# Second attention of a hybrid decoder layer: compressed product with v, and the first query block's local and selected scores, as 256-column joint matmuls

## The chip, the core and the metric

The kernel runs on one core of a Trainium2 chip. The metric is device time in microseconds for one execution; the figure given for a kernel is the median of its runs. Five engines matter here: PE (the matrix engine, whose weight loads have a row of their own, PEld), DVE (vector), ACT (scalar, with the exponential), POOL (GpSimd, which here also issues some DMAs) and SP (which issues most DMAs).

## What is computed

One decoder layer on 512 tokens of width 1024. Three causal token mixers (called DSA, NSA and SSD) work side by side on a common projection, and their gated sum goes through an output projection and a feed-forward block. The change is in the NSA mixer, the second attention. It has 16 query heads in two groups g = 0, 1 of eight heads, each group with its own keys and values, and for each query it adds three attentions with a gate each:

```python
s = jnp.einsum('bqghd,bngd->bqghn', qb, k_cmp) * scale      # compressed: 31 windows
o_cmp = jnp.einsum('bqghn,bngd->bqghd', p_cmp, v_cmp)
s = jnp.einsum('bqghd,bgqkd->bqghk', qb, k_sel) * scale     # selected: 4 blocks of 64 keys
o_slc = jnp.einsum('bqghk,bgqkd->bqghd', p, v_sel)
s = jnp.einsum('bqghd,bkgd->bqghk', qb, kwb) * scale        # local window of 512 keys
o_win = jnp.einsum('bqghk,bkgd->bqghd', p, vwb)
return gb[..., 0:1] * o_cmp + gb[..., 1:2] * o_slc + gb[..., 2:3] * o_win
```

Queries go in four blocks b = 0 to 3 of 128. Keys after the query are masked, so block b needs 128(b+1) keys. For blocks 0 and 1 the four selected key blocks are all that are visible, so the mask of the selected attention is the causal one there.

## The kernel before

**Number format.** A value that has to be exact is split into a high and a low part (`hi`, `lo`), both in a reduced float32 format, and a product is then the sum of two or three matmuls into one PSUM tile. Projections use three of them (`mm3`, L454 to L457); scores use the keys' two parts against one stationary operand that holds the query (`kh` at L905, `kl` at L906); the products with v use the probabilities' two parts (`ph`, `pl`, L956 and L957).

**The attention units.** The NSA work is a list of 32 units (`nsa_units`, L1112): for each pair (b, g) in the order NORD, which is (3,0), (0,0), (2,0), (1,0), (3,1), (2,1), (1,1), (0,1); for each half j = 0, 1 of a group's eight heads, that is four heads; and for each kind, first "w" (local) and then "s" (selected). The keys of the four kinds are separate tiles `K["s0"]`, `K["s1"]`, `K["w0"]`, `K["w1"]` (L514).

**A unit's steps.** `a1` (L893) computes scores: per head two matmuls of n = 128(b+1) columns, then one DVE instruction that copies them out of PSUM, adds the mask and takes the row maximum (L907); after the four heads one small DVE instruction (L912) and four exponentials on ACT (L914). `a2` (L917) divides by the sum and applies the gate. `b1` (L932) transposes the probabilities on PE, 128 keys at a time for four heads (L944), splits them on ACT and DVE (L948, L949) and multiplies them by v (L956, L957, 512 columns: four heads of 128 queries). A "w" unit opens the PSUM tile `pv`, into which `cmp_pv` (L1104) first puts the compressed attention's product with v: one 128-column matmul for each of the four heads (L1108). The "s" unit of the same half adds to the same tile and closes it.

**The pipeline** (L983) runs, for each unit, `load`, `prep`, `a1` of this unit, `b1` of the unit before, `a2` of this unit. A unit's `load` is where the next pair's work is hung in: the loads of its queries (issued by POOL, L1000), its compressed scores (`cmp_a`, L1036), its selection (`cmp_b`) and its transposed compressed probabilities (`cmp_c`).

**The filler and the order.** A second generator, the filler (L691), makes the projections, the merge gates and the branch projections, which are long rows of 512-column matmuls. Each step of the attention yields a number of nanoseconds, times a ratio (2.5 for NSA), and so much filler is traced before the next step (L1759 to L1777). Instructions of the main generator carry a priority that puts them ahead of filler traced up to some thousand steps before (`HM`, L35). A scheduler then orders every engine's instructions at compile time; on the chip each engine runs its list in that order. Near the end some steps wait in this tracing for each other by name: the "s" units of the last pair need the tile `yC` (L1146), and the filler's last NSA branch needs the marks of those units (L1461 to L1474).

Of the kernel before, what the change touches and what calls it, by code (L numbers as in the profile page):

```python
# [7 lines left out]
F32 = mybir.dt.float32  # L8
# [33 lines left out]
def build_kernel(ctx, tc, A, out):  # L42
# [468 lines left out]
    def r_tile(pl, name, shape):  # L511
        return pl.tile(shape, F32R, name=name)

    K = {n: (r_tile(kv, "kh_" + n, [128, S]), r_tile(kv, "kl_" + n, [128, S])) for n in ("s0", "s1", "w0", "w1")}  # L514
    V = {n: r_tile(kv, "v_" + n, [128, NB, 2, 64]) for n in ("s0", "s1", "w0", "w1")}
    mk = popen("mask", side="right")
    K["d"] = (r_tile(mk, "kh_d", [128, S]), r_tile(mk, "kl_d", [128, S]))
# [375 lines left out]
    def a1(u, ratio):  # L893
# [19 lines left out]
        for h in range(4):  # L913
            act.activation(u.p[h][:, :n], u.p[h][:, :n], AF.Exp, bias=u.nb[:, h:h + 1],  # L914
                           scale=rs8[:, u.b, u.h0 + h:u.h0 + h + 1], accum_out=u.sm[:, h:h + 1])

    def a2(u):  # L917
        n = 128 * (u.b + 1)
        rc = at.tile([128, 4], F32, name="rc", bufs=3)
        dve.reciprocal(rc, u.sm)  # L920
        if u.gate is not None:
            dve.tensor_tensor(rc, rc, u.gate, op=ALU.mult)
        for h in range(4):
            if h == 3:
                if u.gate is not None:
                    act.activation(u.p[h][:, :n], u.p[h][:, :n], AF.Copy, scale=rc[:, h:h + 1])
                else:
                    pool.tensor_tensor(u.p[h][:, :n], u.p[h][:, :n], bc(rc[:, h:h + 1], [128, n]), op=ALU.mult)
            else:
                dve.tensor_scalar(u.p[h][:, :n], u.p[h][:, :n], rc[:, h:h + 1], None, op0=ALU.mult)  # L930
# [52 lines left out]
    def pipeline(units, ratio):  # L983
        prev = None
        for u in units + [None]:
            if u is not None:
                if u.load is not None:
                    yield from u.load()
                u.prep()
                yield from a1(u, ratio)  # L990
            if prev is not None:
                yield from b1(prev, ratio)
            if u is not None:
                a2(u)
            prev = u
# [7 lines left out]
    def y_dst(which, h0, b):  # L1003
        t = y_d[which]
        a = t[h0 * 64:(h0 + 4) * 64, b * 128:(b + 1) * 128]
        return a.rearrange("(h d) q -> d h q", d=64)
# [96 lines left out]

    def cmp_pv(b, g, j):  # L1104
        def pre(o, ratio):
            for h in range(4):
                vh = vz[:, g, h % 2].rearrange("p a b -> p (a b)")
                pe.matmul(o[:, h * 128:h * 128 + 128], vh, PC[b, g][:, 2 * j + h // 2], start=h == 0, stop=False)  # L1108
            yield ratio * 428
        return pre  # L1110

    def nsa_units(ratio):  # L1112
# [46 lines left out]
        for i, (b, g) in enumerate(order):  # L1159
            for j in range(2):  # L1160
                for kind in "ws":
                    u = U()
                    u.b, u.h0 = b, 16 + 8 * g + 4 * j
                    u.k, u.v = K[f"{kind}{g}"], V[f"{kind}{g}"]
                    gi = 2 if kind == "w" else 1
                    u.gate = gate[:, b].rearrange("p (h j) -> p h j", j=3)[:, 8 * g + 4 * j:8 * g + 4 * j + 4, gi]
                    u.first, u.last, u.direct = kind == "w", kind == "s", None
                    u.pre = cmp_pv(b, g, j) if kind == "w" else None
                    u.ydst = y_dst("b", 8 * g + 4 * j, b)

                    def prep(u=u, b=b, g=g, j=j, kind=kind):
                        u.q = Q[b, g][j]
                        u.mask = caus[:, 384 - 128 * b:] if kind == "w" else SM[b, g]
                    u.prep = prep
                    u.load = None
                    if i == 0:
                        u.load = {(0, "w"): lambda: start(0), (0, "s"): second, (1, "w"): lambda: start(1),
                                  (1, "s"): lambda: both(1)}[j, kind]
                    elif j == 0 and kind == "w":
                        u.load = lambda i=i: load(i + 1)  # L1180
                        if i == 1:
                            u.load = lambda i=i: att2(load(i + 1))
                    if i and j == 0 and kind == "s":
                        u.load = lambda i=i: cont(i + 1, cmp_q)
                    if i and j == 1 and kind == "w":
                        u.load = lambda i=i: cont(i + 1, cmp_b)
                    if i == 4 and j == 1 and kind == "w":
                        u.load = lambda i=i: mark(cont(i + 1, cmp_b))
                    if i == 7 and kind == "s":
                        u.load = lambda u=u, j=j: direct(u, j)  # L1190
                    elif i == 6 and j == 1 and kind == "s":
                        u.load = lambda i=i: half(cont(i + 1, cmp_c))
                    elif i and j == 1 and kind == "s":
                        u.load = lambda i=i: cont(i + 1, cmp_c)
                    us.append(u)
# [610 lines left out]
```

## Time and profile before

| | |
|---|---|
| median of three runs | 1375.47 us (1375.29 to 1377.54) |
| profiled execution, first to last instruction | 1374.2 us |
| PE busy | 1352.5 us, 98% |
| DVE, ACT, POOL busy | 1001.6, 723.3, 266.7 us |
| first and last score matmul of NSA (L905) | 546.1 and 923.9 us after the start |
| last product with v of NSA (L957) | 956.4 us after the start |

For the profiled execution the page gives the span alone; the median of the runs is 1.3 us above it. A timeline row has a start, a duration and an instruction. Matmuls are pipelined and their ends are modelled, so what a matmul costs is read from the distance between starts, not from its duration.

### The profile page before, as it was taken

The page shows a single profiled execution, that of the slowest core. Times are in us where ns is not written, and L with a number is a line of the kernel's source. Part 1 is how long each engine was busy: PE and PEld are TensorE (multiplying, and loading weights), DVE is VectorE, ACT ScalarE, POOL GpSimd, SP SyncE. Part 2 cuts the span into 40 slices and gives each one's busy share as a digit, 9 for nine tenths or more (in the row PEclk, how much of TensorE's full clock was granted, in tenths as well). Part 3 has the DMA queues.
Part 4 walks back from the last instruction along what each step waited for, and adds up shares of the span by engine and source line. Part 5 has one row for each costly group of instructions (what it writes and reads, how often), then busy time and mean ns, then how long its engine had stood idle before and what let it go on. Part 6 is the DMA issues. An engine that isn't in the chain of part 4 may idle for free.

```text
span 1374.2 us, 19666 instructions
## 1 busy us (share of the span) xinstructions
PE 1352.5 (98%) x6875; PEld 1129.7 (82%) x6875; DVE 1001.6 (73%) x1968; ACT 723.3 (53%) x1434; POOL 266.7 (19%) x230
## 2 busy tenths in 40 slices
PE   9999999999998999999999999999999999999998
PEld 7888888888886767888888888887989888888887
DVE  6499987989877576876676888987745666767741
ACT  5455345676766675566666566553224344443430
POOL 2425111111027783200000001114101201102000
PEclk9999999999999999999999999999999999999999
DMA  6436555554467886635345454546535665846531
GB/s 196 119 91 156 176 162 157 131 140 119 112 215 237 245 252 182 170 104 146 104 115 154 126 147 115 150 138 191 180 112 165 128 167 124 183 113 132 153 119 50
DMA packets 222592, 205.34 MB, mean 149 GB/s; under 512 B 15369, under 2 KB 169885, under 8 KB 222494
## 3 DMA queue, kind: packets, MB, share of 16 engines
q1 hardware_dynamic: 206524, 180.49, 44.8%
q0 software_dynamic: 15232, 20.98, 8.1%
q10 hardware_dynamic: 738, 2.63, 0.5%
q8 instruction: 54, 0.88, 0.3%
q14 instruction: 44, 0.36, 0.1%
HBM read 167.56 MB, written 36.51 MB: 148 GB/s over the span
## 4 chain that ended last, share of the span: by engine, by line
PE 90%; DVE 3%; POOL 2%; DMA 2%; issue 2%; ACT 1%; SPq 0%; DVEq 0%; POOLq 0%; ACTq 0%
PE pj L455 21%; PE pj L456 21%; PE pj L457 21%; PE sc L457 3%; PE sc L455 3%; PE sc L456 3%; PE pT L944 3%; PE sc L906 2%; PE sc L905 2%; PE pv L956 2%; PE pv L957 2%; DMA E<-ac_d 1%; PE pF L944 1%; PE sc L1330 1%; POOL t L1314 1%
## 5 line engine op out<-in xcount | busy, mean ns | idle before, releaser
L172 ACT ACTIVATE whi<-wraw 128x1024 fp32r<-128x1024 f32 (+2 forms) x190 | 198.4, 1047 | 222.4 <-PE pj L456 109.9
L174 DVE TENSOR_TENSOR wlo<-wraw,whi 128x1024 fp32r<-128x1024 f32 (+1 forms) x176 | 226.0, 1287 | 95.4 <-ACT whi L172 93.8
L455 PE MATMUL pj<-hTh,whi 128*128 128x512 f32 x384 | 153.8, 401 | 0.0
L457 PE MATMUL pj<-hTh,wlo 128*128 128x512 f32 x384 | 153.1, 399 | 0.0
L456 PE MATMUL pj<-hTl,whi 128*128 128x512 f32 x384 | 152.8, 398 | 0.0
L914 ACT ACTIVATE p<-p,nb,rs 128x256 f32<-128x256 f32 (+3 forms) x192 | 123.2, 645 | 38.7 <-DVE nb L912 38.6
L455 PE MATMUL pj<-whi,hTh 128*128 128x512 f32 (+2 forms) x336 | 132.0, 393 | 2.6 <-DVE v_s L556 2.2
L456 PE MATMUL pj<-wlo,hTh 128*128 128x512 f32 (+2 forms) x336 | 131.7, 392 | 0.0
L457 PE MATMUL pj<-whi,hTl 128*128 128x512 f32 (+2 forms) x336 | 131.1, 390 | 0.0
L455 PE MATMUL pj<-yh,whi 128*128 128x512 f32 (+1 forms) x288 | 105.9, 374 | 1.9 <-DVE rtok L1535 0.8
L456 PE MATMUL pj<-yl,whi 128*128 128x512 f32 (+1 forms) x288 | 107.4, 373 | 0.0
L457 PE MATMUL pj<-yh,wlo 128*128 128x512 f32 (+1 forms) x288 | 106.6, 370 | 0.0
L456 PE MATMUL pj<-h2l,whi 128*128 128x512 f32 (+1 forms) x256 | 96.3, 376 | 0.0
L457 PE MATMUL pj<-h2h,wlo 128*128 128x512 f32 (+1 forms) x256 | 96.2, 376 | 0.0
L455 PE MATMUL pj<-h2h,whi 128*128 128x512 f32 (+1 forms) x256 | 96.1, 376 | 0.0
L1000 POOL DMA_DIRECT2D qu<-q_d x32 | 23.5, 735 | 330.8 <-PE sc L906 165.4
L457 PEld LDWEIGHTS pj<-hTh,wlo 128*128 128x128 f32 x384 | 72.2, 188 | 14.6 <-issue 0.7
L456 PEld LDWEIGHTS pj<-hTl,whi 128*128 128x128 f32 x384 | 72.3, 188 | 13.5 <-issue 0.7
L455 PEld LDWEIGHTS pj<-hTh,whi 128*128 128x128 f32 x384 | 72.3, 188 | 13.4 <-issue 0.5
L948 ACT ACTIVATE pth<-pT 128x512 fp32r<-128x512 f32 x95 | 55.0, 593 | 49.7 <-PE pT L944 48.1
L455 PEld LDWEIGHTS pj<-whi,hTh 128*128 128x128 f32 x336 | 64.0, 190 | 15.6 <-DVE v_s L556 2.5
L457 PEld LDWEIGHTS pj<-whi,hTl 128*128 128x128 f32 x336 | 63.8, 190 | 12.0 <-issue 0.5
(403 smaller groups left out, 3265.0 us busy)
## 6 DMA issues: line engine op xcount, KB each, us to landing
wraw<-in_w_in_dram SPq DMA_DIRECT2D x84, 512.0 KB, 4.1
wraw<-in_w_ff_dram SPq DMA_DIRECT2D x58, 512.0 KB, 4.3
qd<-in_w_ff_dram POOLq DMA_DIRECT2D x18, 512.0 KB, 5.9
gld<-g_d SPq DMA_DIRECT2D x35, 256.0 KB, 2.7
q_d<-qev SPq DMA_DIRECT2D x64, 128.0 KB, 2.5
qu<-q_d POOLq DMA_DIRECT2D x32, 256.0 KB, 3.8
E<-ac_d SPq DMA_DIRECT2D x16, 512.0 KB, 6.0
xz<-xz_d SPq DMA_DIRECT2D x16, 512.0 KB, 6.0
```

The source lines that it names most:

```text
L172: act.activation(hi[:, :m], r[:, :m], AF.Copy)
L174: (pool if i in LOWP else dve).tensor_tensor(lo[:, :m], r[:, :m], f(hi[:, :m]), op=ALU.subtract)
L455: pe.matmul(o, lh, rh, start=first, stop=False)
L456: pe.matmul(o, lh, rl, start=False, stop=False)
L457: pe.matmul(o, ll, rh, start=False, stop=last)
L905: pe.matmul(s_[:, h % w, :n], u.q[h], kh[:, :n], start=True, stop=False)
L906: pe.matmul(s_[:, h % w, :n], u.q[h], kl[:, :n], start=False, stop=True)
L914: act.activation(u.p[h][:, :n], u.p[h][:, :n], AF.Exp, bias=u.nb[:, h:h + 1], scale=rs8[:, u.b, u.h0 + h:u.h0 + h + 1], accum_out=u.sm[:, ...
L944: pe.transpose(pt[:, h], u.p[h][:, kb * 128:kb * 128 + 128], ident)
L948: act.activation(ph, ptf, AF.Copy)
L956: pe.matmul(o, vk, ph0, start=st, stop=False)
L957: pe.matmul(o, vk, pl0, start=False, stop=en)
```

## The change

Three edits go together.

1. The keys of a group's local and selected attention are laid side by side in one tile, `KJ[g]`, shape 128 x 2 x 512; `K["w0"]` and so on become views of it.
2. For block b = 0, where either kind has 128 keys, the "w" unit calls `a1_two` in place of `a1`: per head two matmuls of 256 columns (128 local and 128 selected keys, two runs 512 elements apart), then two DVE instructions, one for each kind; after the four heads the small DVE instruction and the four exponentials of the "w" unit, then those of the "s" unit. The "s" unit is marked `ready` and skips `a1`. The yields of the two units' scores, 4 x 2 x 2 x 107 ns before the ratio, become 4 x 240 ns.
3. `cmp_pv` makes two matmuls of 256 columns in place of four of 128: two heads that share a stationary operand (the even ones, the odd ones) go together, their output in two runs of 128 columns, 256 apart.

```diff
-    K = {n: (r_tile(kv, "kh_" + n, [128, S]), r_tile(kv, "kl_" + n, [128, S])) for n in ("s0", "s1", "w0", "w1")}
+    KJ = [(r_tile(kv, f"kh_j{g}", [128, 2, S]), r_tile(kv, f"kl_j{g}", [128, 2, S])) for g in range(2)]
+    K = {f"{n}{g}": tuple(t[:, i] for t in KJ[g]) for i, n in enumerate("ws") for g in range(2)}
...
+    def a1_two(u, v, ratio):
+        for w in (u, v):
+            for n in ("mx", "nb", "sm"):
+                setattr(w, n, at.tile([128, 4], F32, name={"sm": "smx"}.get(n, n), bufs=3))
+            t = at.tile([128, 4, 128], F32, name="p", bufs=PB)
+            w.p = [t[:, h] for h in range(4)]
+        for h in range(4):
+            if h % 2 == 0:
+                s_ = ps("sc", [128, 2, 2, 128])
+            for i, k in enumerate(u.two):
+                pe.matmul(s_[:, h % 2], u.q[h], k[:, :, :128], start=i == 0, stop=i == 1)
+            for i, w in enumerate((u, v)):
+                dve.tensor_tensor_reduce(w.p[h], s_[:, h % 2, i], caus[:, 384:], 1.0, -3.4e38, ALU.add, ALU.max,
+                                         accum_out=w.mx[:, h:h + 1])
+            yield ratio * 240
+        rs = rs8[:, u.b, u.h0:u.h0 + 4]
+        for w in (u, v):
+            dve.scalar_tensor_tensor(w.nb, w.mx, -1.0, rs, op0=ALU.mult, op1=ALU.mult)
+            for h in range(4):
+                act.activation(w.p[h], w.p[h], AF.Exp, bias=w.nb[:, h:h + 1], scale=rs[:, h:h + 1], accum_out=w.sm[:, h:h + 1])
...
-                yield from a1(u, ratio)
+                if getattr(u, "two", None) is not None:
+                    yield from a1_two(u, units[units.index(u) + 1], ratio)
+                elif not getattr(u, "ready", False):
+                    yield from a1(u, ratio)
...
-            for h in range(4):
-                vh = vz[:, g, h % 2].rearrange("p a b -> p (a b)")
-                pe.matmul(o[:, h * 128:h * 128 + 128], vh, PC[b, g][:, 2 * j + h // 2], start=h == 0, stop=False)
+            o4 = o.rearrange("p (k e q) -> p e k q", k=2, e=2)
+            for e in range(2):
+                vh = vz[:, g, e].rearrange("p a b -> p (a b)")
+                pe.matmul(o4[:, e], vh, PC[b, g][:, 2 * j:2 * j + 2], start=e == 0, stop=False)
...
+                    u.two = KJ[g] if b == 0 and kind == "w" else None
+                    u.ready = b == 0 and kind == "s"
...
-                        u.mask = caus[:, 384 - 128 * b:] if kind == "w" else SM[b, g]
+                        u.mask = caus[:, 384 - 128 * b:] if kind == "w" or u.ready else SM[b, g]
```

## The prediction

> **What bounds the kernel now.** I read the page's first part, then the table by stage, then the list of what PE waited for while the second attention (NSA) runs.
>
> ```profile
> span 1374.2 us, 19666 instructions
> PE 1352.5 (98%) x6875; PEld 1129.7 (82%) x6875; DVE 1001.6 (73%) x1968; ACT 723.3 (53%) x1434; POOL 266.7 (19%) x230
> ```
> ```profile
> core 0: us, PE busy (x) PEld busy (x) DVE busy (x) ACT busy (x) POOL busy (x), PEclk, DMA share, GB/s
> 545.00:600.00 55.00, 54.96 (x282) 45.56 (x280) 41.86 (x102) 31.84 (x63) 13.39 (x6) 1.00 0.59 163
> 600.00:640.00 40.00, 40.00 (x214) 33.62 (x214) 26.70 (x83) 22.86 (x49) 0.71 (x1) 1.00 0.40 110
> ...
> 880.00:940.00 60.00, 60.00 (x301) 49.93 (x300) 48.26 (x122) 34.31 (x82) 11.24 (x8) 1.00 0.52 154
> 940.00:1000.00 60.00, 58.12 (x343) 50.82 (x342) 44.06 (x69) 18.37 (x25) 14.55 (x9) 1.00 0.62 206
> ```
> ```profile
> PE pj L455 <- DVE rtok L1535: 0.8, 1, 0.8
> PE pj L455 <- ACT yh L820: 0.7, 1, 0.7
> PE pj L455 <- DVE gld L1535: 0.4, 1, 0.4
> PE pj L455 <- DVE x L1564: 0.3, 1, 0.3
> ```
>
> The third fence is the whole list of PE's waits from 545 to 1010 us: 0.8 + 0.7 + 0.4 + 0.3 = 2.2 us. PE's busy time alone would prove little, since the ends of matmuls are modelled; the short list does. The attention's short pieces lie inside the filler's long rows of 512-column matmuls, and PE goes from one to the next without a pause. DVE is busy 48.26 of 60 us and ACT 34.31 where the last query blocks run, 26.70 and 22.86 of 40 us where the first pair with b = 0 runs: neither is the bound, nor are the DMAs at 0.40 to 0.62. The granted clock is 1.00. So time in this stage is the sum of what PE's matmuls cost, and one that goes away shortens the kernel wherever in the stage it stands.
>
> **Which matmuls the change touches.** All of line 1108, and those of lines 905 and 906 that have 128 columns and read a kind "w" or "s" key:
>
> ```profile
> L1108 PE MATMUL pv<-cph,vz 128*128 128x128 f32 x64 | 9.6, 267 | 0.0
> ```
> ```profile
> L905 PE MATMUL sc<-kh_w,qu x64: 218/333/478, 546.1 to 912.4; 128*128 128x512 f32 x16, 128*128 128x128 f32 x16, 128*128 128x384 f32 x16, 128*128 128x256 f32 x16
> L905 PE MATMUL sc<-kh_s,qu x64: 220/337/442, 559.3 to 923.9; 128*128 128x512 f32 x16, 128*128 128x128 f32 x16, 128*128 128x384 f32 x16, 128*128 128x256 f32 x16
> ```
> ```profile
> L906 PE MATMUL sc<-kl_w,qu x64: 273/309/400, 546.4 to 912.5; 128*128 128x512 f32 x16, 128*128 128x128 f32 x16, 128*128 128x384 f32 x16, 128*128 128x256 f32 x16
> L906 PE MATMUL sc<-kl_s,qu x64: 273/332/459, 559.5 to 923.9; 128*128 128x512 f32 x16, 128*128 128x128 f32 x16, 128*128 128x384 f32 x16, 128*128 128x256 f32 x16
> ```
>
> That is 64 products with v and 4 x 16 = 64 score matmuls, 128 in all, each of 128 columns. The change replaces them by 64 of 256 columns. Counted in groups of four that become two: 16 groups of products (one for each "w" unit) and 16 groups of scores (a head's four matmuls), 32 groups.
>
> **What a matmul of each width costs.** The durations in these rows (267 ns, 273 ns) hold the passage through the array, which overlaps the next one; the cost is the distance between starts. One place of the timeline has eight of the short ones in a row:
>
> ```profile
> 906.61 0.40 PE L457 MATMUL pj<-yh,wlo 128*128 128x512 f32 x1
> 906.84 0.40 PE L455 MATMUL pj<-yh,whi 128*128 128x512 f32 x1
> 907.07 0.22 PE L905 MATMUL sc<-kh_s,qu 128*128 128x128 f32 x1
> 907.13 0.28 PE L905 MATMUL sc<-kh_w,qu 128*128 128x128 f32 x1
> 907.24 0.28 PE L906 MATMUL sc<-kl_s,qu 128*128 128x128 f32 x1
> 907.36 0.27 PE L906 MATMUL sc<-kl_w,qu 128*128 128x128 f32 x1
> 907.47 0.61 PE L1108 MATMUL pv<-cph,vz 128*128 128x128 f32 x4
> 907.91 0.44 PE L456 MATMUL pj<-yl,whi 128*128 128x512 f32 x1
> 908.20 0.39 PE L457 MATMUL pj<-yh,wlo 128*128 128x512 f32 x1
> ```
>
> A 512-column matmul costs 906.84 - 906.61 = 0.23 us. From 907.07 to 908.20 there are 1.13 us for eight short ones and one long: (1.13 - 0.23) / 8 = 0.1125 us for a short one. The first appears to cost only 0.06 (907.07 to 907.13), but the long one behind the row takes 908.20 - 907.91 = 0.29 instead of 0.23: the 0.06 that were missing are paid there. Something of about 0.11 us that does not depend on the columns goes with each matmul; I read it as the load of its own stationary operand, which each of them has, and which a 512-column matmul hides and a 128-column one does not.
>
> A 256-column matmul stands in the scores of query block 1, between long ones:
>
> ```profile
> 883.46 0.28 PE L905 MATMUL sc<-kh_s,qu 128*128 128x256 f32 x1
> 883.58 0.28 PE L906 MATMUL sc<-kl_s,qu 128*128 128x256 f32 x1
> 883.70 0.39 PE L456 MATMUL pj<-yl,whi 128*128 128x512 f32 x1
> 883.93 0.39 PE L957 MATMUL pv<-ptl,v_s 128*128 128x512 f32 x1
> ```
>
> 883.46 to 883.70 is 0.24 us for two, 0.12 us each, and the long one behind takes its usual 0.23: nothing is left over. So 256 columns cost hardly more than 128.
>
> **The sum.** A group costs 4 x 0.1125 = 0.45 us before and 2 x 0.12 = 0.24 us after: 0.21 us saved. 32 groups: 6.7 us, half of it from the products with v, half from the scores. Against the profiled execution that is 1374.2 - 6.7 = 1367.5 us of span. The median of the runs is 1375.47 - 1374.2 = 1.3 us above the span, and I keep that: 1368.8 us.
>
> The Trainium skill ("TensorE: Matmul & The Clock Gate", section "Back-to-back issue gap") gives for a stream of weight loads and matmuls about 81 ns at 128 columns and 131 ns at 512. With an estimate of 98 ns between them at 256, a group would save 4 x 81 - 2 x 98 = 128 ns and the kernel 4.1 us. The rows above have 112 and 230 ns in their place, and the trace decides.
>
> **What is not on PE.** DVE and ACT keep their instructions: eight mask-and-maximum instructions, two small ones and eight exponentials for the two units, on the same 128 x 128 shapes. Their cost is nothing as long as PE has filler to run, which in this stage it has. No DMA is added. What moves: the "s" unit's four mask-and-maximum instructions and four exponentials now stand ahead of the transposes' copies for the unit before, and behind the "w" unit's first scores. DVE has in queue behind them the copies out of PSUM for `b1`; ACT the other half of these. The loads of the next queries on POOL wait for the last score matmul that reads a query buffer, and that one comes earlier. The keys' joint tile is written long before 545 us, in two parts as before; I cost it at nothing. The smaller yields trace 4 x (428 - 240) x 2.5 = 1880 ns less filler for each of the four joint units; since PE is filled either way, this shifts where filler stands, and I cost it at nothing too. If PE had no filler there, the price would be the rival below.
>
> Two shapes of operands are not in the trace: a moving operand in two runs of 128 columns 512 elements apart (scores), and an output in two runs 256 apart (products). Their bounds are 0.12 us, the 256-column row, and 2 x 0.1125 = 0.225 us, two short matmuls; I take 0.12, as the row of the same count of columns. A gain below 0.12 is excluded to within 0.005, because two such matmuls fill the 0.23 us of one with 512 columns.
>
> **The rivals.**
>
> *The two runs cost what two matmuls cost.* Then 64 x 0.225 us equal 128 x 0.1125 us and nothing is gained: 1375.5. For it speaks only that no row shows such an operand; against it that the 0.11 us go with a matmul's own weights, and one load serves both runs.
>
> *Cost goes by columns.* If the 0.1125 us were an accident of the one row that I read, and a matmul really cost its columns, 0.23 / 512 = 0.45 ns each, then four times 128 columns would be twice 256 columns, 0.23 us both, and nothing would be gained: 1375.5. The 0.06 us between 907.07 and 907.13 is just that rate; the seven distances behind it are double. The same section of the Trainium skill has this rule for a single matmul, columns over 2.4 plus 2.5 ns, 55.8 and 109.2 ns; by it a group would save 5 ns and the kernel 0.2 us, and the trace disagrees with 112 for 128 columns.
>
> *The gain turns into waits on loads.* After NSA the filler's rows wait for y to be fetched and split (the 0.7 and 0.8 us rows above, and 60 - 58.12 = 1.9 us of idle PE from 940 to 1000). If transfers there do not start earlier, PE arrives sooner and waits longer. With these waits doubled, 1.9 us are lost: 1370.7. Against it: the buffers that these transfers need are freed by PE's own progress.
>
> *Slower: the "w" unit's softmax comes late.* Between its scores and its transposes there used to stand the scores of the "s" unit; now the joint scores come first, and the exponentials start only after eight mask-and-maximum instructions in place of four, with eight exponentials ahead of the copies for `b1`.
>
> ```profile
> L907 DVE CUSTOM_DVE_ANT_0 p<-sc,caus 128x128 f32<-128x128 f32 x48 | 13.5, 285 | 13.4 <-PE sc L906 12.9 <-PE pT L944 0.3
> L907 DVE DVE_READ_ACCUMULATOR2_ANT mx<- 128x1 f32 x192 | 15.6, 81 | 0.0
> ```
> ```profile
> L914 ACT ACTIVATE p<-p,nb,rs 128x128 f32<-128x128 f32 x48 | 23.1, 483 | 9.3 <-DVE nb L912 9.3
> ```
>
> Four times 285 + 81 ns are 1.5 us on DVE, four times 483 ns are 1.9 us on ACT, and the 0.9 us of the "s" unit's eight score matmuls no longer lie in between: up to 4.3 us for each of four joint units, 17.2 us, if PE's list puts the transposes where they would have been ready and no filler ahead of them. 1375.5 - 6.7 + 17.2 = 1386.0. It decides from 6.7 / 4 = 1.7 us of PE waiting in each joint unit. For it speaks that PE's order is fixed at compile time; against it that the same kind of wait is absent today: in the list of waits none of PE's is for line 914 or 948, and in the row of line 907 it is DVE that waits for PE.
>
> **How the numbers follow.** I give the forecast 0.72, the gain partly turned into waits 0.09 (two thirds of it still more than 0.2% faster), two runs as two matmuls 0.06, cost by columns 0.04, slower 0.09. About 0.2%, 2.7 us, is what a measurement of this kernel can tell from no change. Faster: 0.72 + 0.06 = 0.78. Same: 0.03 + 0.06 + 0.04 = 0.13. Slower: 0.09. The time is that of the forecast, 1368.8. Downward the range allows for all of the 2.2 us of waits to vanish with the new order (1366.6), and half a microsecond for the widths read to 0.01 us: 1366.0. Upward it reaches to no gain, 1375.5. It leaves out the slower case and the rims of the others, under 2 in 10. The forecast's own range is 1366.0 to 1371.5.
>
> **What would show it right or wrong.** PE should have 64 matmuls fewer, 6811. Line 1108's successor should show two 256-column matmuls in 0.24 us, and the long matmul behind them at 0.23; the joint scores the same. If these distances are 0.2 us or more, the rival of the two runs holds. The list of PE's waits from 545 to 1000 us should stay near 2 us; a row of waits for line 914's successor, for 948 or for 949, of 1.7 us or more per joint unit, would be the slower case. NSA's last product with v and everything behind it should come about 6.7 us earlier, and the stretches before 545 us should be unchanged; a difference there would be a new order, not this change's arithmetic.

## The result and the profile after

The changed kernel takes 1384.72 us (median of four runs, 1382.92 to 1386.15) beside 1375.84 us (1375.29 to 1377.54) for the kernel before on the same chip: a ratio of 1.006, with a 95% interval of 1.0046 to 1.0074. It is slower by 8.9 us, where 6.7 us less had been forecast. The profiled execution took 1384.38 us, 1.7 us more than its span.

The page's first part, and the table by stage for the stretches that the prediction showed:

```profile
span 1382.7 us, 19544 instructions
PE 1354.4 (98%) x6811; PEld 1125.4 (81%) x6811; DVE 996.7 (72%) x1968; ACT 722.2 (52%) x1434; POOL 272.3 (20%) x230
```
```profile
545.00:600.00 55.00, 55.00 (x280) 45.94 (x279) 40.06 (x101) 30.89 (x61) 13.05 (x6) 1.00 0.58 161
600.00:640.00 40.00, 40.00 (x212) 33.63 (x211) 31.22 (x109) 28.61 (x71) 1.43 (x2) 1.00 0.42 119
640.00:880.00 240.00, 237.69 (x1228) 199.62 (x1228) 180.12 (x463) 146.72 (x312) 15.49 (x14) 1.00 0.45 127
880.00:940.00 60.00, 54.86 (x241) 41.40 (x240) 41.26 (x103) 27.61 (x64) 13.90 (x8) 1.00 0.44 133
940.00:1000.00 60.00, 56.73 (x328) 48.85 (x327) 44.73 (x70) 19.42 (x27) 16.47 (x10) 0.97 0.56 183
```

PE has the 64 matmuls fewer (6811). Up to 640 us it is as full as before. From 640 to 880 us it is idle for 2.3 us, and from 880 to 940 us for 5.1; before, it had no idle time at all in either. The row of before for 640 to 880 us, which the prediction does not show:

```profile
640.00:880.00 240.00, 240.00 (x1252) 202.82 (x1251) 186.14 (x477) 148.33 (x316) 16.35 (x16) 1.00 0.46 130
```

The list of PE's waits from 545 to 1010 us had four rows and 2.2 us. Now it has ten (columns as before: total, times, longest):

```profile
PE pj L455 <- ACT yh L821: 4.6, 5, 2.5
PE pv L1134 <- DVE yt L996: 1.3, 1, 1.3
PE pv L978 <- ACT pth L970: 1.2, 2, 0.8
PE pj L455 <- DVE gld L1565: 1.1, 2, 0.8
PE pF L966 <- DVE p L952: 0.9, 1, 0.9
PE pj L455 <- DVE rtok L1563: 0.8, 1, 0.8
PE sc L928 <- DVE mx L930: 0.3, 1, 0.3
PE pj L455 <- DVE x L1592: 0.3, 1, 0.3
PE pv L979 <- DVE ptl L971: 0.2, 1, 0.2
PE pj L456 <- DVE yl L822: 0.2, 1, 0.2
```

Together 10.9 us. The largest row is the filler's: its matmuls (L455) wait for a y tile to be split (L821), which is the first step of a new branch. The matmuls themselves cost what was forecast. Two places of PE's timeline, the joint scores and the joint product:

```profile
612.17 0.40 PE L928 MATMUL sc<-kh_j,qu 128*128 128x256 f32 x2
612.41 0.40 PE L928 MATMUL sc<-kl_j,qu 128*128 128x256 f32 x2
612.65 0.39 PE L978 MATMUL pv<-pth,v_w 128*128 128x512 f32 x1
612.88 0.40 PE L455 MATMUL pj<-hTh,whi 128*128 128x512 f32 x1
...
882.83 0.40 PE L1134 MATMUL pv<-cph,vz 128*128 128x256 f32 x2
883.07 0.40 PE L978 MATMUL pv<-pth,v_w 128*128 128x512 f32 x1
883.30 0.28 PE L928 MATMUL sc<-kh_j,qu 128*128 128x256 f32 x1
```

612.17 to 612.65 is 0.48 us for four, 882.83 to 883.07 is 0.24 us for two: 0.12 us each, and the 512-column matmuls behind keep their 0.23. Of the 64 joint matmuls, 53 are followed by the next matmul after 0.112 to 0.124 us; the distances behind the other 11, 0.149 to 1.06 us, hold waits or leftovers of their neighbours.

**A ledger.** To see where the saving went, I add up matmul widths between 545 us and the end of the first NSA branch (the start of DVE's last merge in it). A matmul of n columns is put at 0.4427 ns a column plus 1 ns, and at 111 ns at least; these fit the distances read in the prediction, 0.23 and 0.1125 us. What the trace takes beyond the sum is called lost: pauses, and slower matmuls. So "attention" is a count of matmuls at fixed prices, and "lost" is all that remains; neither is measured by itself. The filler's branches are, in order, the DSA branch a0, the two halves of SSD c0 and c1, and the first NSA branch b0.

| us | merge gates | a0 | c0 | c1 | b0 | sum |
|---|---|---|---|---|---|---|
| attention, before | 68.5 | 27.3 | 21.1 | 12.3 | 1.4 | 130.5 |
| attention, after | 66.9 | 27.2 | 23.8 | 4.3 | 1.1 | 123.3 |
| lost, before | 1.7 | 0.9 | 0.8 | 1.0 | 1.9 | 6.4 |
| lost, after | 1.8 | 1.9 | 5.3 | 8.7 | 4.8 | 22.5 |

By this count the attention's matmuls take 7.2 us less. The lost time grows by 16.1 us, and 10.6 of these lie in c1 and b0; 16.1 - 7.2 = 8.9 us, 0.4 more than the spans differ by (1382.7 - 1374.2 = 8.5). Behind b0 the time is the same (409.1 us in both), and NSA's first matmul starts at 545.1 us instead of 545.8.

The attention's scores now finish early. The small DVE instruction that ends a unit's scores stands in one row before, in two after:

```profile
L912 DVE SCALAR_TENSOR_TENSOR nb<-mx,rs x32: 147/157/726, 562.3 to 926.1; 128x4 f32<-128x4 f32 x32
```
```profile
L913 DVE SCALAR_TENSOR_TENSOR nb<-mx,rs x24: 106/161/447, 562.4 to 876.4; 128x4 f32<-128x4 f32 x24
L935 DVE SCALAR_TENSOR_TENSOR nb<-mx,rs x8: 144/156/164, 613.6 to 896.4; 128x4 f32<-128x4 f32 x8
```

The last one starts at 896.4 instead of 926.1 us. (The last product with v does not come earlier: it starts in b0, at 964.9 us instead of 956.4.) So in c1 there are 4.3 us of attention where there were 12.3, and where a branch ends and the next one's y is not there yet, PE has nothing else in its list. The longest pause is at the start of b0. SP's, ACT's and PE's rows for it:

```profile
944.94 0.32 SPq L1447 DMA_DIRECT2D gld<-g_d  x1
945.36 0.38 SPq L153 DMA_DIRECT2D wraw<-in_w_br_nsa_dram  x1
945.80 0.97 SPq L820 DMA_DIRECT2D yr<-yb_d  x2
```
```profile
950.17 1.36 ACT L821 ACTIVATE yh<-yr 128x512 fp32r<-128x512 f32 x2 [3.89 <-DMA yr<-yb_d]
```
```profile
947.98 0.40 PE L457 MATMUL pj<-yh,wlo 128*128 128x512 f32 x1
950.85 0.74 PE L455 MATMUL pj<-yh,whi 128*128 128x512 f32 x2 [2.48 <-ACT yh L821]
```

The third and fourth y tile are asked for at 945.80, behind 256 KB of gates and 512 KB of weights, and land 4.3 us later; PE stands from 948.2, where the 0.23 us of the matmul at 947.98 end, to 950.85: 2.65 us. (The row's 2.48 counts from that matmul's modelled end.)

### The profile page after: what moved, and what is told of

Its sections match the earlier page's. It is cut to its first block, busy times and chain, and to the rows that moved or that the text cites. A ratio compares the mean times of both kernels' runs of the same rounds, so it can differ in the third digit from the quotient of the medians.

```text
span 1382.7 us, 19544 instructions
## 1 busy us (share of the span) xinstructions
PE 1354.4 (98%) x6811; PEld 1125.4 (81%) x6811; DVE 996.7 (72%) x1968; ACT 722.2 (52%) x1434; POOL 272.3 (20%) x230
## 4 chain that ended last, share of the span: by engine, by line
PE 79%; DVE 6%; DMA 5%; POOL 4%; ACT 3%; issue 2%; SPq 0%; DVEq 0%; POOLq 0%; ACTq 0%
PE pj L455 19%; PE pj L456 19%; PE pj L457 19%; PE sc L457 3%; PE sc L456 3%; PE sc L455 3%; PE pT L966 2%; PE sc L907 2%; PE pv L978 2%; PE sc L906 2%; PE pv L979 2%; DMA E<-ac_d 1%; DMA yr<-yc_d 1%; POOL E L1318 1%; POOL xz L1330 1%
## 5 line engine op out<-in xcount | busy, mean ns | idle before, releaser
L455 PE MATMUL pj<-hTh,whi 128*128 128x512 f32 x384 | 153.2, 399 | 0.0
L455 PE MATMUL pj<-whi,hTh 128*128 128x512 f32 (+2 forms) x336 | 131.5, 391 | 2.8 <-DVE v_s L557 2.2
L915 ACT ACTIVATE p<-p,nb,rs 128x256 f32<-128x256 f32 (+3 forms) x160 | 107.8, 677 | 42.2 <-DVE nb L913 42.2
L455 PE MATMUL pj<-yh,whi 128*128 128x512 f32 (+1 forms) x288 | 106.6, 375 | 6.5 <-ACT yh L821 4.6
L455 PE MATMUL pj<-h2h,whi 128*128 128x512 f32 (+1 forms) x256 | 96.1, 376 | 0.0
L455 PEld LDWEIGHTS pj<-hTh,whi 128*128 128x128 f32 x384 | 72.2, 188 | 13.6 <-issue 0.5
L455 PEld LDWEIGHTS pj<-whi,hTh 128*128 128x128 f32 x336 | 63.6, 189 | 15.0 <-DVE v_s L557 2.5
```

Source lines behind the costliest of these rows:

```text
L455: pe.matmul(o, lh, rh, start=first, stop=False)
```

## Experiments

All ratios are to the kernel before, run beside it on the same chip, with 95% intervals. "Lost" and "attention" are sums of the ledger, each from the one profiled execution. That one lies up to 2.9 us from the median of its kernel (2.9 above it with the joint scores alone, the slowest of six), so two lost times that differ by less than about 3 us are not told apart.

**First: each part alone, and the yields.** The joint product without the joint scores, as an edit of the kernel before:

```diff
-            for h in range(4):
-                vh = vz[:, g, h % 2].rearrange("p a b -> p (a b)")
-                pe.matmul(o[:, h * 128:h * 128 + 128], vh, PC[b, g][:, 2 * j + h // 2], start=h == 0, stop=False)
+            o4 = o.rearrange("p (k e q) -> p e k q", k=2, e=2)
+            for e in range(2):
+                vh = vz[:, g, e].rearrange("p a b -> p (a b)")
+                pe.matmul(o4[:, e], vh, PC[b, g][:, 2 * j:2 * j + 2], start=e == 0, stop=False)
```

> The kernel before with the joint product with v alone (32 matmuls of 256 columns for 64 of 128); scores and yields as before. Order theory (the smaller yields of the joint scores let the attention run ahead of the filler, so that it is used up where the filler has its gaps): the yields are untouched, so the saving shows in full, 16 x 0.21 = 3.4 us, 1372.4 us. Late-softmax theory (the joint scores with their eight exponentials make PE wait): the same, 1372.4. Any-change theory (each edit gives another order with losses of its own): no saving, 1376 to 1385.

1380.02 us, 1.0015 (1.0006 to 1.0025). The saving of 3.4 us does not show; 13.6 us are lost instead of 6.4.

The joint scores without the joint product, as an edit of the changed kernel:

```diff
-            for e in range(2):
-                vh = vz[:, g, e].rearrange("p a b -> p (a b)")
-                pe.matmul(o4[:, e], vh, PC[b, g][:, 2 * j:2 * j + 2], start=e == 0, stop=False)
+            for h in range(4):
+                vh = vz[:, g, h % 2].rearrange("p a b -> p (a b)")
+                pe.matmul(o[:, h * 128:h * 128 + 128], vh, PC[b, g][:, 2 * j + h // 2], start=h == 0, stop=False)
```

> The changed kernel with the old product with v: joint scores and their small yields alone. Order theory and late-softmax theory alike: all of the loss is here, 1384.7 + 3.4 = 1388 us. Any-change theory: anything between 1372 and 1388.

1388.24 us, 1.0077 (1.0064 to 1.0091). The worst of the four: 0.6 us of attention are left in c1, 25.5 us are lost. The change with the yields of before:

```diff
-            yield ratio * 240
+            yield ratio * 428
```

> The changed kernel with the yield of the joint scores set to 428 per head, so that the two units together yield what the separate ones did. All matmuls are those of the change. Order theory: the attention keeps its old place beside the filler, PE's lost time from 746 to 1000 us goes from 23 us back to about 7, and the time is 1369 us, at most 1373. Late-softmax theory: nothing about the joint scores has changed, 1384 us. Any-change theory: between.

1384.77 us, 1.0053 (1.004 to 1.0066). The last small DVE instruction of the scores still starts at 894.4 us, so the smaller yields are not what makes the scores early; that theory falls. The kernel before, with no matmul touched, and only smaller yields for the scores of block 0:

```diff
-            yield ratio * max(n / 2.4, 107) * 2
+            yield ratio * (120 if u.b == 0 and u.k is not K["d"] else max(n / 2.4, 107) * 2)
```

> The kernel before, its matmuls untouched, but with block 0's NSA scores yielding 120 per head and unit in place of 214, so that the two units together yield the 240 per head of the change. Order theory: the attention runs ahead as in the changed kernel, and the kernel is slower by up to 16 us, 1380 to 1391. Late-softmax theory: no change, 1375.8. Any-change theory: anything from 1373 to 1385.

1383.32 us, 1.0042 (1.0028 to 1.0055): slower by about 5 us with the same work. The two largest of its five rows of waits are of the same kind as the change's largest:

```profile
PE pj L455 <- ACT yh L820: 3.8, 2, 3.4
PE pj L456 <- DVE yl L821: 1.6, 2, 1.4
```

So an edit that only makes the scheduler write a new order can cost more than half of what the change costs (1.0042 beside 1.006), and no joint matmul is needed for that.

**Second: the order held, and the attention held back.** In two kernels every instruction gets its rank in the order of before as its priority:

```diff
-    pe, act, dve, pool = nc.tensor, nc.scalar, nc.vector, nc.gpsimd
+    pe, act, dve, pool = Px(nc.tensor, "T"), Px(nc.scalar, "A"), Px(nc.vector, "V"), Px(nc.gpsimd, "P")
...
+                tc.cur_priority = RANK[key][o] * 8 if FIX[0] is None else FIX[0]
```

> The product with v alone as joint matmuls, and the order of before written into the priorities: every instruction of the program gets its rank in the order of before as its priority in the scheduler, so that the compile-time order stays near that of before (the lists still differ in places). The last attention instructions then stand in the rows of the second SSD branch as before (15.0 us of attention after the first half of the SSD rows by matmul widths; before 12.2 there, counted in the same way). Theory 'cover' (the saving on PE is real, and time is lost where a new order leaves PE's loads of y uncovered): the saving of 3.4 us appears, ratio to before 0.9975, that is 1372 to 1373 us beside 1376. Rival 'any new order loses' (the order of before is a lucky one, and any difference costs): 1.001 to 1.004 as in the run with the joint product alone. Rival 'joint matmuls cost more than they show' (PE time of the joint product is hidden in the modelled ends): no gain, 1.000 or above.

> The whole change (yields of 428 a head), with the order of before written into the priorities as in the run beside it; the mask-and-maximum instructions of the selected kind rank right behind those of the local kind. By matmul widths 10.1 us of attention stand behind the first half of the SSD rows (after the change 4.7, before 12.2). Theory 'cover': the saving of 6.7 us appears less what the joint softmax costs by waiting, ratio 0.995 to 0.998, that is 1369 to 1373 beside 1376. Rival 'any new order loses': 1.003 to 1.006. Rival 'joint softmax late' (the slower rival of the prediction, independent of where the attention stands): 1.000 to 1.005, with PE waits for the lines 930, 942 to 952 of several us.

The product alone: 1381.68 us, 1.003 (1.0018 to 1.0042), 16.9 us lost. The whole change, with its old yields: 1379.26 us, 1.0018 (1.0005 to 1.003), 16.7 lost. Both miss what "cover" expected. They have 11.2 and 9.5 us of attention in c1, and c1 and b0 lose 7.3 and 7.2 us instead of 13.5; but c0 loses 6.6 and 6.7, with new waits of up to 1.7 us of scores for the row maximum that frees their PSUM tile. Here, priorities taken from an order did not give that order.

The other two hold the attention back by one line, once in the change and once in the kernel before:

```diff
+        HI[0] = 400
         yield from pipeline(nsa_units(R2), R2)
```

> The whole change, and one line more: the priority offset of the second attention's instructions is 400 in place of 4000, so that attention pieces are no longer always put ahead of the filler. By matmul widths 15.9 us of attention then stand in the second SSD branch's rows (after 4.7, before 12.2), some of them up to the first NSA branch rows. Theory 'cover': lost time of PE in these stretches falls from 21 us to about 7, ratio to before 0.993 to 0.998 (1367 to 1373 beside 1376). Rival 'any new order loses': 1.003 to 1.006 as for the other new orders. Rival 'joint softmax late': 1.000 to 1.005, with PE waiting for DVE and ACT at the joint units.

> The kernel before, matmuls untouched, with the priority offset of 400 in place of 4000 in the second attention: a new order, with 13.4 us of attention in the second SSD branch's rows (before 12.2), reaching further towards the first NSA branch. Theory 'cover': 0.998 to 1.001, since the cover is the same or a little better. Rival 'any new order loses': 1.003 to 1.006.

The change: 1374.38 us, 0.9981 (0.9969 to 0.9993), faster than the kernel before by 0.2%, about the least that the prediction called measurable. The kernel before with the same line: 1384.14 us, 1.0044 (1.0024 to 1.0064). Between these two, whose texts differ by the change alone (their orders differ too), it is 0.9981 / 1.0044 = 0.994, 9.8 us between their medians. That pair has lost times of 12.7 and 14.2 us, nearly the same, and so the saving shows, in this one pair of orders. "Cover" gave the sign for the first, though it expected about 7 us lost and not 12.7; for the second it expected level and was wrong, and the rival "any new order loses" (1.003 to 1.006) was right: the scheduler's new list also lost 5.3 us in c0. PE's waits in the faster kernel:

```profile
PE pj L455 <- ACT yh L821: 3.8, 3, 2.2
PE pj L455 <- DVE rtok L1563: 0.7, 1, 0.7
PE pj L455 <- DVE gld L1563: 0.4, 1, 0.4
PE pj L455 <- DVE x L1592: 0.3, 1, 0.3
PE sc L1066 <- DMA qu<-q_d: 0.3, 1, 0.3
```

All waits for the attention's own softmax are gone from the list; the waits for y remain.

**Third: without the loads, and other offsets.** The second SSD branch and the first NSA branch reuse the y tiles of the branch ahead, in both kernels:

```diff
             elif br == "b0":
-                Y = load(br, range(4), "B")
+                Y = Y[:4]
...
-            else:
+            elif br == "c0":
                 Y = load(br, range(k0, k0 + 4), "A") + load(br, range(k0 + 4, k0 + 8), "B")
```

> The kernel before, with the loads of y for the second SSD branch and for the first NSA branch left out (their rows reuse the y tiles of the branch ahead, so the output is not the layer's). PE's list is that of before up to the second SSD branch. Theory 'cover' (what the changed kernel loses, it loses where PE waits for y to be fetched and split between branches, once the attention has run out): before has little to lose there, 4.5 us in the NSA branches' rows, so 2 to 4 us go, ratio 0.997 to 0.9985. Rival 'any new order loses' : 1.000 or above.

> The change, with the same two sets of loads left out (output not the layer's). PE's list is that of after up to the second SSD branch. Theory 'cover': the 8.7 us lost in the second SSD branch's rows and most of the 7.4 us behind go, with the 1.7 us of half clock at 952 to 956 us; the first SSD branch's 5.3 us stay. 10 to 13 us less than after, 1370 to 1373, ratio to before 0.995 to 0.9985, and below or level with the unchanged kernel without these loads. Rival 'joint softmax late or dearer joint matmuls': the loss stays where the joint units are, ratio 1.003 or above, and 4 us or more above the unchanged kernel without these loads.

The kernel before without the loads: 1380.18 us, 1.0022 (1.0007 to 1.0037). The change without them: 1379.1 us, 1.0012 (1.000 to 1.0024). PE's list was the same as with the loads up to c1, so the stretch is the test. PE's whole list of waits from 880 to 960 us in the change without the loads:

```profile
PE pF L966 <- DVE p L952: 0.5, 1, 0.5
```

With as little attention in c1 (4.4 us), c1 and b0 lose 1.6 us instead of 13.5. So what the change lost there hangs on fetching and splitting y: that is shown. (Loads and splits, on ACT and DVE, are gone together, and the change's waits for gates and for the attention's own lines in this stretch went with them; which part counts is not told by this.) At the end of b0 the change is 4.0 us ahead in the two profiled executions (960.0 against 964.0 us); but these lie 1.9 us below and 1.8 us above their medians, which are only 1.1 us apart, so this pair does not show the saving itself. The totals miss their numbers because the next loads were not ready either: in both kernels the last branches, which took 409.1 us to the end, now take 416.3 and 415.5, with pauses of 1.6 and 2.1 us for their own y and a clock below 1.00 behind them that costs 3.4 and 1.7 us. In the change, b0 ends 13.6 us earlier than with the loads, and 6.4 of these are handed back behind it, where the next loads are not ready.

The change with two other offsets, 300 and 0, each the one line above with its number:

> The whole change with a priority offset of 300 for the second attention in place of 4000 (400 gave 0.9981). By matmul widths 19.5 us of attention stand in the second SSD branch's rows and 5.6 in the first NSA branch's. Theory 'cover': the wait at the start of the NSA branch goes too, 0.995 to 0.998. Rival 'any new order loses': the order is as good as drawn, 0.998 to 1.006.

> The whole change with no priority offset for the second attention. By matmul widths 15.6 us of attention stand in the second SSD branch's rows and 12.0 in the rows of the first NSA branch, and the last NSA branch has to wait for the end of the attention. Theory 'cover': the waits between branches are covered, but the end of the attention comes late for the last NSA branch: 0.996 to 1.002. Rival 'any new order loses': 1.002 to 1.006.

300 gives 1383.55 us, 1.0047 (1.003 to 1.0064): 17.6 us of attention in c1, and yet a pause of 3.2 us at 873 us; 22.0 us are lost. 0 gives 1385.51 us, 1.0051 (1.0034 to 1.0069): only 9.3 us are lost up to the end of b0, but the last 15 us of attention then stand behind b0, ahead of the last NSA branch, and from b0 to the end it takes 441.0 us instead of 409.1. So more attention in c1 did not by itself make up for the pauses.

**Fourth: mending the loads with PE's order kept.** The first NSA branch takes its y tiles from the pool that is free earlier; PE's list stays that of the kernel it is made from, but for one line in the one with the offset:

```diff
-                Y = load(br, range(4), "B")
+                Y = load(br, range(4), "A")
...
             if br == "c1":
+                pclose("yB")
+            if br == "b0":
                 pclose("yA")
...
-        pclose("yB")
```

> The change, with one thing about buffers: the first NSA branch takes its y tiles from pool A, which the second SSD branch has finished with 2.7 us before its end, in place of pool B, whose tiles it reads to the end; pool B is closed in its place. The order of the matmuls stays that of after, instruction for instruction; DVE's list differs in 2 lines, ACT's in 22, SP's in none. Theory 'cover' (the losses are waits for y between branches that no attention covers): the pause of 2.65 us at 951 us and the stretch at half clock behind it (1.7 us) go, 3 to 4.5 us, ratio 1.003 to 1.004. Rival 'the transfers themselves are late' (the loads queue behind a weight transfer on the same DMA engines, whatever buffer they go to): under 1.5 us, ratio 1.005 to 1.006.

> The change, the priority offset of 400, and the first NSA branch's y in pool A. The order of the matmuls is that of the run with the offset alone but for one line. There 2.8 us were lost in the first NSA branch's rows. Theory 'cover': 1 to 2 us of them go, ratio to before 0.9965 to 0.9975, about 1372 beside 1376. Rival 'the transfers themselves are late': 0.998, as with the offset alone.

> The kernel before with the first NSA branch's y in pool A, nothing else. Before loses 1.9 us in the first NSA branch's rows and has no pause over 0.9 us there. Theory 'cover': 0.5 to 1.5 us go, ratio 0.999 to 1.000, much less than the 3 to 4.5 us of the changed kernel. Rival 'the transfers themselves are late': 1.000.

1390.27 us, 1.0093 (1.0075 to 1.0112); 1379.85 us, 1.0022 (1.0006 to 1.0038); 1381.3 us, 1.0032 (1.0018 to 1.0046). By the ratios, each is 4 to 6 us slower than the kernel it is made from. The pause at b0 stays (2.78 us in the change): the tiles of pool B were not what it waited for. And the pool closed early let 2.5 MB for the next stage start 24 us sooner, in front of the gates of the last branch. ACT's rows and DVE's wait in the kernel before with pool A:

```profile
965.98 0.37 ACTq L1557 DMA_DIRECT2D g2b<-in_norm_g_dram  x1
966.39 2.78 ACTq L1560 DMA_DIRECT2D xin<-in_x_dram  x4
```
```profile
DVE gld L1535 <- DMA gld<-g_d: 4.9, 2, 3.9
```

They ran at 989.6 us before. A gate tile (256 KB) lands 6.0 us after its issue instead of 3.5 (medians from 964 to 980 us), and the last branches take 412.2 us instead of 409.1.

The last three move the four loads to POOL's queue and hold the 2.5 MB back to their old place:

```diff
-            nc.sync.dma_start(yr, y_d[br[0]][kk * 128:kk * 128 + 128])
+            (pool if br == "b0" else nc.sync).dma_start(yr, y_d[br[0]][kk * 128:kk * 128 + 128])
...
+            with tc.issue_after(MH):
                 act.dma_start(xin[:, t], dram(A["x"], t * 128 * D, [[D, 128], [1, D]]))
```

> The change; the first NSA branch's y in pool A as before; its four loads issued from POOL's queue, where they no longer stand behind SP's loads of gates and weights; and the 2.5 MB for the next stage held in ACT's list behind the fifth instruction of line 1568, where they ran before. The order of the matmuls is that of after but for 6 lines. Theory 'the transfers are late' (what the run with pool A alone left standing: the wait at 951 us is the time from issue to landing of the third and fourth y tile behind a gate and a weight transfer on SP's queue): the pause of 2.7 us shrinks to under 1.3 and the half clock behind it goes, and the 3.3 us lost in the last branch to the early loads come back; ratio 1.002 to 1.0035. Rival 'a new order as such': no gain over after, 1.0055 or above.

> The change with the priority offset of 400 and the same mends. Theory 'the transfers are late': 1 to 2 us below the run with the offset alone (0.9981), 0.9965 to 0.9975. Rival: 0.998 or above.

> The kernel before with the same mends, its matmuls in the order of before but for 6 lines. Its rows of the first NSA branch lose 1.9 us. Theory 'the transfers are late': 0.5 to 1.5 us gained, 0.999 to 0.9995. Rival: 1.000.

1384.11 us, 1.0063 (1.0042 to 1.0084); 1384.62 us, 1.0043 (1.0025 to 1.006); 1376.69 us, 0.9999 (0.9988 to 1.001). The side effect is gone (408.9 us to the end in each). The pause is not: 2.74 us in the change, and 4.61 in the kernel with the offset. SP's queue was not the reason either: issued from POOL's queue, the third and fourth tile land 4.5 and 4.3 us after their issue (medians, in the change and in the kernel with the offset), no sooner than the 4.3 us that they took behind the gates and weights on SP's queue. What delays their issue stands in DVE's and POOL's rows in the change with these mends:

```profile
939.69 0.69 DVE L1556 SCALAR_TENSOR_TENSOR gld<-gld,rtok 128x512 f32<-128x512 f32 x1 [3.90 <-DMA gld<-g_d]
940.30 0.68 DVE L1565 TENSOR_TENSOR gld<-gld,pj 128x512 f32<-128x512 f32 x1
940.89 1.22 DVE L174 TENSOR_TENSOR wlo<-wraw,whi 128x1024 fp32r<-128x1024 f32 x1
942.03 2.38 DVE L822 TENSOR_TENSOR yl<-yr,yh 128x512 fp32r<-128x512 f32 x2
```
```profile
944.11 1.14 POOL L820 DMA_DIRECT2D yr<-yb_d  x2 [0.84 <-DVE yl L822]
```

ACT split the first two tiles from 939.18 to 940.46 us; DVE's half (L822) stands in its list behind the merge of the branch ahead, which waited 3.90 us for a gate, and only L822 frees the buffer that the third tile is loaded into. In the kernel with the offset L822 was done at 943.85 us, and there the loads stood behind a merge in POOL's own list until 946.09. Whether the pause would go if buffer, queue and the order of DVE and POOL were mended together was not tried.

| us | ratio | attention | of it in c1 | lost to end of b0 | of it in c1, b0 |
|---|---|---|---|---|---|
| before | 1 | 130.5 | 12.3 | 6.4 | 2.9 |
| before, smaller yields | 1.0042 | 130.5 | 12.3 | 14.2 | 9.8 |
| before, offset 400 | 1.0044 | 130.5 | 17.4 | 14.2 | 5.4 |
| product alone | 1.0015 | 126.2 | 15.2 | 13.6 | 8.5 |
| scores alone | 1.0077 | 127.1 | 0.6 | 25.5 | 16.8 |
| the change | 1.006 | 123.3 | 4.3 | 22.5 | 13.5 |
| the change, old yields | 1.0053 | 122.5 | 3.6 | 20.9 | 15.4 |
| the change, order of before as priorities | 1.0018 | 123.6 | 9.5 | 16.7 | 7.2 |
| the change, offset 400 | 0.9981 | 122.3 | 15.4 | 12.7 | 7.2 |

The span less the two sums (attention and lost) is 1236.4 to 1238.1 us in every row: the filler's matmuls and the time outside the ledger change by less than 2 us. (A few matmul records can be missing from a trace, so attention sums of kernels with the same matmuls differ by up to 1.3 us.)

## Why the prediction was wrong

- **What a matmul costs, and the sum: right.** 0.12 us for 256 columns, in two runs of 128 as much as in one; 7.2 us less attention by widths, forecast 6.7. Both rivals that made the gain vanish on PE (two runs as two matmuls, cost by columns) are refuted.
- **"Time in this stage is the sum of what PE's matmuls cost, and one that goes away shortens the kernel wherever in the stage it stands", and with it that what shifts costs nothing, "since PE is filled either way": this step failed.** The list of waits showed that PE was full under the order of before, and I took that for a property of the stage. It belongs to that order: the change loses 22.5 us there in place of 6.4, and two other orders of the matmuls of before lose 14.2. The smaller yields, of which the second sentence speaks, are not the reason: with the old ones 20.9 us are lost. Of the 16.1 us more, 10.6 lie in c1 and b0, and with the loads and splits of y left out nearly all of what is lost there goes (1.6 us instead of 13.5).
- **I also had the cover the wrong way round, as far as the runs tell.** Filler was to hide the attention's waits; in c1 and b0 the attention's pieces seem to hide the filler's waits for y. The change ends the attention's scores 29.7 us earlier and leaves 4.3 of 12.3 us of attention in c1. All five kernels whose attention in c1 was under 5 us and which loaded their y lost 13.5 to 16.8 us in c1 and b0; those with 9.5 us or more lost 2.9 to 12.2. This is a pattern over runs and no proof: all five have the joint scores in them, and the kernel before with smaller yields lost 9.8 us there with the same 12.3 us of attention in c1.
- **The rival "the gain turns into waits on loads" named the right place and sized it wrongly.** It doubled the 1.9 us of idle PE that the order of before showed; c1 and b0 lost 13.5 us, 10.6 more than before. (Of the two rows of 0.7 and 0.8 us that it reads as waits for y, only the 0.7 is one; the 0.8, `rtok` at L1535, is a merge that reads a gate tile.) Its counter-argument, that PE's own progress frees the buffers, missed the split on DVE, which frees the buffer of the third tile, and the 4.3 us from its issue to its landing.
- **The slower rival had the sign and not the mechanism.** PE's waits for the softmax's lines (970, 952, 930, 971) add up to 2.6 us in all, not 1.7 us and more in each of four joint units.
- **What would show it:** the stretches before 545 us are unchanged to within 0.7 us, as said. The waits were to stay near 2 us, and were 10.9. NSA's last product with v was to come about 6.7 us earlier, and came 8.4 us later.

Open is why the joint scores let the attention's scores run ahead (the yields are excluded; that a pair of block 0's units now shares two PSUM tiles, where each unit had one of its own, was not tried alone), and what part of the loss would remain in a typical order of the changed kernel. The 4.5 us more that are lost in c0 hold waits of the attention's own lines (978 for 970, 966 for 952), which no run isolates.

## What to carry to other kernels

Where a scheduler writes the order at compile time, the trace of one kernel is one draw: a saving of 0.5% on the bounding engine is here of the size of what a new order costs (0.42 and 0.44% with the same matmuls), and it is tested by comparing the change under several orders (here one more line in both kernels), not by one. Before costing displaced work at nothing, ask which stalls it hides now: look for the places where the long-running stream changes its operands, and for who fills PE there. Here a load was only as early as the last in-order list that its buffer, or its issue, passed through.

## What the hardware showed beside this

A pause of PE costs more than its length. The table by single microseconds around the pause at b0 in the changed kernel (the clock granted to PE is the third number from the right):

```profile
949.00:950.00 1.00, 0.00 (x0) 0.00 (x0) 0.00 (x0) 0.00 (x0) 0.00 (x0) 1.00 0.90 328
950.00:951.00 1.00, 0.15 (x1) 0.15 (x2) 0.17 (x1) 0.73 (x2) 0.00 (x0) 1.00 0.85 242
951.00:952.00 1.00, 1.00 (x4) 0.53 (x5) 0.96 (x2) 0.53 (x1) 0.00 (x0) 1.00 1.00 358
952.00:953.00 1.00, 1.00 (x5) 0.81 (x4) 0.26 (x1) 0.00 (x0) 0.00 (x0) 0.74 0.73 229
953.00:954.00 1.00, 1.00 (x4) 0.71 (x4) 0.00 (x0) 0.00 (x0) 0.00 (x0) 0.50 0.87 293
954.00:955.00 1.00, 1.00 (x4) 0.66 (x2) 0.28 (x1) 0.00 (x0) 0.00 (x0) 0.50 0.63 203
955.00:956.00 1.00, 1.00 (x4) 0.51 (x3) 0.83 (x2) 0.91 (x1) 0.52 (x1) 0.56 0.07 17
956.00:957.00 1.00, 1.00 (x6) 0.84 (x5) 1.00 (x2) 0.78 (x2) 1.00 (x2) 1.00 0.03 11
```

PE works again from 950.85 us, and from about 952.5 its clock is 0.50 for 3.4 us: 0.26 + 0.50 + 0.50 + 0.44 = 1.7 us more, of the 4.8 lost in b0. The length of a pause (the distance between two starts less the first one's width) does not decide it alone: half clock followed pauses of 1.82, 1.84 and 1.88 us in other kernels here, and did not follow ones of 1.61, 1.86, 2.29, 2.40 and 2.70 us.

The rows of the granted clock show what does. In each of the 20 traces, all its changes after the first 10 us lie whole multiples of 3.413 us apart, to within 0.002 us. If PE's idle time (distances between starts, less the widths of the ledger) is summed in each of these stretches of 3.413 us between 545 and 1365 us, those at half clock left out, then the 21 stretches with 2.09 us or more were each followed by one at half clock, and none of the others, with up to 2.03 us, was. So a pause that falls across the end of a stretch counts in two parts, and short pauses in one stretch add up: with offset 300 the clock fell at 941.7 us without any pause above 1.2 us ahead of it, after 2.35 us of idle time in the stretch.

The Trainium skill ("TensorE: Matmul & The Clock Gate", "Part 1: The HAM clock gate") has a free-running window of about 3.4 us after which an idle array is throttled to half. The stretches of 3.413 us agree with that; that a window need not be idle throughout is what these runs add. The rule that the Trainium skill has in the same page's section "HAM oscillation — how this bites in real kernels", no idle gaps over about 3.4 us, is too generous by these runs: a pause of 1.82 us was enough, in a stretch with 2.26 us of idle time.
